# A hybrid SSD and pooling decoder block: the ssd gate as four Strassen pairs, adaLN rows called in other stages, four more warm-up matmuls

## The chip, the cores and the metric

One core of one Trainium2 chip runs the whole block. The metric is the device time of one execution in microseconds, the median of three runs. Beside it there is the profile of one execution, whose span is a little shorter than its own device time.

## What is computed

One decoder block on a sequence of 512 tokens with 1024 channels, all in float32. Cut to what matters here:

```python
mod = silu(c) @ w_ada + b_ada                       # 6 x 1024: shift, scale, gate, twice
h = rmsnorm(x) * (1 + scale_m) + shift_m
z, xbc, dt, u_pool, gate_logits = split(h @ w_in)
y = ssd_scan(silu(conv(xbc)), dt) * silu(z)         # 4 groups, chunks of 128 tokens
y_ssd = group_rmsnorm(y) @ w_branch_ssd
y_pool = causal_pool(u_pool) @ w_branch_pool
g_ssd, g_pool = split(sigmoid(gate_logits))
x = x + gate_m * ((g_ssd * y_ssd + g_pool * y_pool) @ w_out)
h = rmsnorm(x) * (1 + scale_f) + shift_f
x = x + gate_f * (relu(h @ w_up)**2 @ w_down)
out = rmsnorm(x)
```

The gates are 2 x 1024 columns of `h @ w_in`: "the pool gate" and "the ssd gate" below. They are the two halves of the last part of `w_in`.

## The kernel before, in words

Everything is kept transposed: a tile has 128 channels on the partitions and the 512 tokens along the row. Each float32 operand is split into `hi` and `lo` (both float32r): ScalarE copies `hi` (L125, L145, L833), VectorE subtracts `lo` (L126, L146, L834). A product is then three matmuls, hi·hi, hi·lo and lo·hi, in `mm3` (L155, L156, L157). A `unit` makes one output tile of 128 channels: 8 blocks of K times 3 matmuls of 512 columns, 24 in all. Its weights come by `load_unit` (L140 to L146): one DMA of 512 KB on SP's queue into one of 4 `RAW` buffers, then a cast and a subtraction into two of the `HL` buffers.

The stages, in order on TensorE:

1. **First norm** (L200 to L333, an order written out by hand). 12 warm-up matmuls (`warm`, L215 to L221) run while x arrives; two float32 matmuls (L242) broadcast silu(c); three (L251) sum the squares of x; five more warm-up matmuls follow; then the first eight output tiles are summed for each arriving block of h (L321, L327). On the way from the sums to the first L327 lie ScalarE's L295 and L296 (the reciprocal root), VectorE's L312 and ScalarE's L315. `ada(j)` (L171) is one row of `silu(c) @ w_ada`: a DMA of 512 KB from `adaT` and one product-sum on VectorE. Rows 0 to 15 are made here.
2. **Scan**, groups 0 to 3. `run` interleaves the steps of one group's scan with `unit`s that fill TensorE: the convolution's inputs of the next group (`u_x`, `u_bc`, `u_z`) and the branch product of the group before (`bs`, four loads and eight output tiles). At a group's end its y is normalised by L595 and split by L126. Group 3 is filled with the pooling inputs (`pool_in`, L630 to L634) and `pool_mix`.
3. **Pool gate**: 8 units with a sigmoid (L702); after the fourth come `bs(3, i)`, which need the y of group 3, and the second `pool_mix`.
4. **Pool branch**: 8 units of `w_branch_pool`, each multiplied onto the gate (L719).
5. **Ssd gate**: 8 units of h with a sigmoid (L727), times the branch sum (L729), plus the pool part (L730), split (L126) into `mg`.
6. **Output projection**: 8 units of `w_out` on `mg` (five whole, three in halves of 256 tokens), the residual (L759), the second norm in halves (L776, L805 to L807).
7. **MLP** in four quarters. The last three quarters of `w_up` are already done as Strassen pairs (`class Pair`, L886; its matmuls are L892): two output tiles together by seven products of 4 blocks of K times 3 matmuls of 256 columns, 84 matmuls in place of 48 of 512 columns. `prepare` (L853) makes a pair's weight sums on VectorE: four additions of 512 columns, three subtractions of 1024 and one of 512 for `lo`. `sums` (L835) makes the sums of the moving side. L924 and L930 add in PSUM.

The 32 remaining rows of adaLN (16 to 47) are `ada_next` calls: one after each pool gate, one after each `bs(3, i)`, two after each pool branch unit, and the last four in the ssd gate.

A scheduler orders each engine's queue from the program; loads under `urgent` are pulled ahead. Each queue then runs strictly in the order given: on VectorE a waiting instruction holds all behind it. Buffers rotate: a `RAW` buffer's next DMA waits until both the cast and the subtraction (or the L171) that read it are done.

Of the kernel before, what the change touches and what calls it, by code (L numbers as in the profile page):

```python
# [62 lines left out]
def block_kernel(tc, xp, crow, arow, par, adaT, wstart, wz, wx, wpool_in, wgate, wpw, wbs, wbp, wout, wup, wdn, out):  # L63
# [3 lines left out]
    with (  # L67
# [54 lines left out]
        def split(src):  # L122

            hi, lo = S.get(F32R), S.get(F32R)
            act.copy(hi, src)  # L125
            done[0] = dve.tensor_tensor(lo, src, hi.bitcast(F32), ALU.subtract)  # L126
# [98 lines left out]
        with tc.manual_schedule():  # L225
# [17 lines left out]
            HL.put(wide)  # L243
            ps = PU.get()
# [188 lines left out]
        def u_z(g, i):  # L433
            def f():
# [5 lines left out]
                PU.put(ps)  # L440
            return f
# [257 lines left out]
        for j in range(8):
            gp = F.get()  # L700
            ps = unit(wgate[8 + j], h)
            behind(act.activation(gp, ps, AF.Sigmoid))  # L702
            PU.put(ps)
            merged.append(gp)
            if j == 1:
                for _ in rest:
# [16 lines left out]
        mg = []
        for j in range(8):
            gs = F.get()
            ps = unit(wgate[j], h)
            last = act.activation(gs, ps, AF.Sigmoid)  # L727
# [1 line left out]
            dve.tensor_tensor(gs, gs, acc[j], ALU.mult)  # L729
# [7 lines left out]
        free(h)
        with tc.issue_after(last.ins):
            table = act.preload_act_table_set("natural_log_exp_and_others")

        for p_, t in zip((XS, SZ, XS, SZ), later):
            p_.put(t)
        xbig = [XS.get(), XS.get()]
        later = [SZ.get(), SZ.get()]
        F = Slots(lambda i, dt: later[i // 4][:, i % 4, :], 8)


        x1 = []
# [62 lines left out]

# [376 lines left out]
```

## Time and profile before

| | us |
|---|---|
| median of three runs | 967.13 |
| the three runs | 967.13, 965.73, 967.98 |
| the profiled execution's own time | 967.31 |
| its span in the profile | 965.6 |
| TensorE busy | 950.9 |
| VectorE busy | 657.7 |
| ScalarE busy | 500.3 |

A row of the timeline reads: start, duration, engine, line, operation, output<-inputs, size, count, and in brackets the idle time of the engine just before and what ended it. PE is TensorE, DVE VectorE, ACT ScalarE, POOL GpSimd, SP the queue of the DMAs. Matmuls overlap, so their rate is read from the distance of starts and not from one's duration.

### The profile page before, as it was taken

What the parts mean: (1) busy time and instruction counts of PE and PEld (TensorE: products, weight loads), DVE (VectorE), ACT (ScalarE), POOL (GpSimd) and SP (SyncE); (2) the same over time, 40 slices, a digit from 0 to 9 for tenths busy, and PEclk for the clock granted to TensorE, in tenths of its full rate; (3) what the DMA queues carried; (4) which work ended last, traced back from release to release, by engine and by line L of the source; (5) the groups of instructions that cost most, each with busy time, mean ns of one, the idle gap of its engine ahead of it and who ended that gap; (6) DMA issues with size and microseconds to landing.
All of it is one profiled execution on the core that took longest, in us unless ns stands there. A gap on an engine that the chain in (4) does not pass through costs nothing.

```text
span 965.6 us, 13253 instructions
## 1 busy us (share of the span) xinstructions
PE 950.9 (98%) x5131; PEld 803.7 (83%) x5131; DVE 657.7 (68%) x961; ACT 500.3 (52%) x811; POOL 89.7 (9%) x91
## 2 busy tenths in 40 slices
PE   7999999999999999999999999999999999999996
PEld 4877788888888888787888888998899889889986
DVE  7978869567866787987576574795557556664633
ACT  5479976567527642563412452684157137425732
POOL 0102320320312132300000000000000000000000
PEclk9999999999999999999999999999999999999998
DMA  9746333432253333446578453242144225214002
GB/s 355 303 131 181 114 124 118 133 110 94 84 154 116 94 114 126 158 153 202 176 266 270 125 206 113 101 144 68 52 142 132 66 75 165 86 35 152 25 1 88
DMA packets 61761, 129.22 MB, mean 134 GB/s; under 512 B 4673, under 2 KB 29505, under 8 KB 61698
## 3 DMA queue, kind: packets, MB, share of 16 engines
q1 hardware_dynamic: 61696, 128.38, 40.9%
q8 instruction: 40, 0.66, 0.3%
q14 instruction: 23, 0.19, 0.1%
q10 hardware_dynamic: 2, 0.00, 0.0%
HBM read 126.13 MB, written 2.23 MB: 133 GB/s over the span
## 4 chain that ended last, share of the span: by engine, by line
PE 84%; DVE 8%; DMA 3%; ACT 2%; issue 1%; POOL 0%; SPq 0%; DVEq 0%; ACTq 0%; POOLq 0%
PE ps L155 21%; PE ps L156 21%; PE ps L157 21%; PE ps L892 12%; PE ps L327 4%; DMA d<-cs_d 2%; DVE d L146 2%; PE ps L548 1%; DVE s L126 1%; PE ps L528 1%; DMA d<-xp 1%; DVE pad L630 1%; DVE s L396 1%; DVE d L171 1%; PE ps L502 1%
## 5 line engine op out<-in xcount | busy, mean ns | idle before, releaser
L155 PE MATMUL ps<-s,d 128*128 128x512 f32 (+1 forms) x1080 | 412.2, 382 | 1.6 <-ACT sz L438 0.6
L156 PE MATMUL ps<-s,d 128*128 128x512 f32 (+1 forms) x1080 | 408.2, 378 | 0.2 <-DVE s L126 0.2
L157 PE MATMUL ps<-s,d 128*128 128x512 f32 (+1 forms) x1080 | 408.1, 378 | 0.0
L155 PEld LDWEIGHTS ps<-s,d 128*128 128x128 f32 x1080 | 202.6, 188 | 42.9 <-issue 2.1
L157 PEld LDWEIGHTS ps<-s,d 128*128 128x128 f32 x1080 | 202.7, 188 | 38.3 <-issue 0.2
L156 PEld LDWEIGHTS ps<-s,d 128*128 128x128 f32 x1080 | 202.8, 188 | 37.4 <-DVE s L126 0.7
L146 DVE TENSOR_TENSOR d<-d,d 128x1024 fp32r<-128x1024 f32 x88 | 112.2, 1275 | 61.2 <-ACT d L145 56.3
L145 ACT CAST d<-d 128x1024 fp32r<-128x1024 f32 x88 | 92.2, 1048 | 115.6 <-PE ps L156 80.5
L892 PE MATMUL ps<-s,d 128*128 128x256 f32 x864 | 103.8, 279 | 0.0
L892 PEld LDWEIGHTS ps<-s,d 128*128 128x128 f32 x864 | 102.9, 188 | 0.2
L833 ACT CAST d<-d 128x1024 fp32r<-128x1024 f32 x44 | 45.9, 1052 | 88.5 <-PE ps L156 62.7
L834 DVE TENSOR_TENSOR d<-d,d 128x1024 fp32r<-128x1024 f32 x44 | 53.5, 1224 | 27.4 <-ACT d L833 16.8
L833 ACT CAST d<-sz 128x1024 fp32r<-128x1024 f32 x32 | 33.7, 1053 | 68.9 <-PE ps L156 48.9
L1081 DVE SCALAR_TENSOR_TENSOR xs<-ps,mod,xs 128x512 f32<-128x512 f32 x29 | 21.8, 750 | 69.6 <-PE ps L157 69.6
L171 DVE CUSTOM_DVE_ANT_0 d<-d,d,par_t 128x1024 f32<-128x1024 f32 x32 | 41.8, 1306 | 26.7 <-DMA d<-adaT 26.6
L834 DVE TENSOR_TENSOR d<-sz,d 128x1024 fp32r<-128x1024 f32 x32 | 39.2, 1224 | 19.8 <-ACT d L833 18.4
L498 ACT ACTIVATE d<-d,ncs 128x128 f32<-128x128 f32 x128 | 40.0, 393 | 3.6 <-POOL d L494 3.5
L327 PE MATMUL ps<-s,d 128*128 128x512 f32 x168 | 40.1, 391 | 1.6 <-ACT s L315 1.6
L396 DVE SCALAR_TENSOR_TENSOR s<-ps,par_t,s 128x511 f32<-128x511 f32 (+2 forms) x54 | 39.6, 741 | 0.3
L327 PEld LDWEIGHTS ps<-s,d 128*128 128x128 f32 x168 | 31.4, 188 | 9.3 <-ACT s L315 2.1
L125 ACT CAST s<-s 128x512 fp32r<-128x512 f32 x32 | 19.8, 621 | 31.1 <-POOL s L510 18.7
L126 DVE TENSOR_TENSOR s<-s,s 128x512 fp32r<-128x512 f32 x32 | 25.7, 805 | 4.8 <-ACT s L125 4.8
(219 smaller groups left out, 1005.0 us busy)
## 6 DMA issues: line engine op xcount, KB each, us to landing
d<-adaT SPq DMA_DIRECT2D x32, 512.0 KB, 4.1
d<-wx SPq DMA_DIRECT2D x18, 512.0 KB, 3.6
d<-wdn SPq DMA_DIRECT2D x18, 512.0 KB, 3.8
d<-cs_d SPq DMA_DIRECT2D x16, 512.0 KB, 6.0
d<-wbs SPq DMA_DIRECT2D x16, 512.0 KB, 3.5
d<-wgate SPq DMA_DIRECT2D x16, 512.0 KB, 4.4
d<-wz SPq DMA_DIRECT2D x15, 512.0 KB, 3.5
sz<-wdn SPq DMA_DIRECT2D x14, 512.0 KB, 3.9
```

The costliest lines, as they stand in the source:

```text
L145: act.copy(hi[:, :w], r[:, a:a + w])
L146: (low or dve).tensor_tensor(lo[:, :w], r[:, a:a + w], hi[:, :w].bitcast(F32), ALU.subtract)
L155: pe.matmul(ps, whi, xhi[:, t0:t1], start=start, stop=False)
L156: pe.matmul(ps, whi, xlo[:, t0:t1], start=False, stop=False)
L157: pe.matmul(ps, wlo, xhi[:, t0:t1], start=False, stop=stop)
L171: dve.tensor_tensor_reduce(r, r, cbc, 1.0, col("b_ada", j), ALU.mult, ALU.add, mod[:, j:j + 1])
L327: pe.matmul(first[u], w[u][i // 2], h[k][i % 2], start=k == 0 and i == 0, stop=k == 7 and i == 2)
L396: dve.scalar_tensor_tensor(t[:, sh:], ps[:, :T - sh], w(3 - sh), t[:, sh:], ALU.mult, ALU.add)
L498: act.activation(m[:, i, :], m[:, i, :], AF.Exp, bias=ncs[:, c, g * HG + i:g * HG + i + 1])
L833: act.copy(dst[0], src)
L834: dve.tensor_tensor(dst[1], src, dst[0].bitcast(F32), ALU.subtract)
L892: pe.matmul(ps, x, y, start=start and m == 0 and i == 0, stop=m == 3 and i == 2, skip_group_check=True)
```

## The change

**The ssd gate** becomes four Strassen pairs over h. The functions for pairs move up in the file so that the gates can use them; `run_jobs(gates)` runs the four pairs, and the first one's weights are prepared ahead, in the pool branch. Needed for it: the sums of h (`whole`), made from `hi + lo` during the pool branch; `gated`, which does sigmoid, product, sum and split for one output tile; weights of the ssd gate laid out in pairs on the host (`wgs`). Three `HL` buffers more are free from the second pool gate on (the scan's `MT`).

**The adaLN rows** are called elsewhere: one after each `bs` of groups 0 and 1 and after each `u_z` of groups 2 and 3 (16 rows), one after each pool gate (8), two after each of the first whole units of the output projection (8). None is left in the pool branch and in the ssd gate.

**Warm-ups**: `warm(4)` between the broadcast of silu(c) and the sums of squares.

```diff
+            warm(4)
             ps = PU.get()
             sq = [HL.get() for _ in range(4)]
...
+                if g > 1:
+                    ada_next()
...
+                if g < 2:
+                    ada_next()
...
-            ps = unit(wgate[8 + j], h)
+            ps = unit(wgate[j], h)
...
-                F.free += range(12, 16)
+                HL.free += range(8, 11)
...
                 for i in range(4):
                     bs(3, i)()
-                    ada_next()
                 pool_mix(1)()
...
+        def whole(m):
+            us = [U.get(), U.get()]
+            for u, (hi, lo) in zip(us, h[2 * m:2 * m + 2]):
+                dve.tensor_tensor(u, hi.bitcast(F32), lo.bitcast(F32), ALU.add)
...
+            sums(*us, *ts)
+        def gated(p, i, ps, sign):
+            gs = U.get()
+            n = T // len(ps)
+            for i_, part in enumerate(ps):
+                done[0] = act.activation(gs[:, n * i_:n * (i_ + 1)], part, AF.Sigmoid, scale=float(sign))
+            j = 2 * p + i
             dve.tensor_tensor(gs, gs, acc[j], ALU.mult)
             dve.tensor_tensor(gs, gs, merged[j], ALU.add)
...
             mg.append(split(gs))
...
         for j in range(8):
             ps = unit(wbp[j], pout)
             dve.tensor_tensor(merged[j], merged[j], ps, ALU.mult)
             PU.put(ps)
-            ada_next(2)
...
+            if j < 4:
+                ht.append(whole(j))
+            if j == 4:
...
+                hb = moving(h, ht)
+                gates = [Pair(wgs[p], hb, lambda i, ps, sign, p=p: gated(p, i, ps, sign)) for p in range(4)]
+                gates[0].prepare()
...
-        for j in range(8):
-            gs = F.get()
-            ps = unit(wgate[j], h)
-            last = act.activation(gs, ps, AF.Sigmoid)
...
-            if rows:
-                ada_next()
+        run_jobs(gates)
+        last = done[0]
...
             ps = unit(wout[j], mg)
             residual(ps, j, 16)
             PU.put(ps)
+            ada_next(min(2, len(rows)))
```

What this does to the queues, at three places. First TensorE's queue at the first norm; L242 is the broadcast of silu(c), L251 (now L252) the sums of squares, L220 a warm-up. Before:

```order
L242 MATMUL ps_18_128<-d_17_125,ones 128x512
L242 MATMUL ps_19_129<-d_17_125,ones 128x512
L251 MATMUL ps_20_132<-d_22_134,ones 128x512
L251 MATMUL ps_20_132<-d_23_135,ones 128x512
L251 MATMUL ps_20_132<-d_24_136,ones 128x512
L220 LDWEIGHTS s_6_85
L220 MATMUL ps_25_153<-s_6_85 128x512
```

Now:

```order
L242 MATMUL ps_18_128<-d_17_125,ones 128x512
L242 MATMUL ps_19_129<-d_17_125,ones 128x512
L220 LDWEIGHTS s_6_85
L220 MATMUL ps_20_132<-s_6_85 128x512
...
L252 MATMUL ps_21_137<-d_23_139,ones 128x512
L252 MATMUL ps_21_137<-d_24_140,ones 128x512
L252 MATMUL ps_21_137<-d_25_141,ones 128x512
```

Four warm-ups stand ahead of the sums; nothing else of TensorE's order moves before the ssd gate.

Second, VectorE's queue just ahead of the normalising of group 3's y (L595, now L600) in the pool gate; L634 (L639) is the last step of a pooling input, L171 an adaLN row, L146 a weight's `lo`. Before:

```order
L171 ISA d_714_3990,mod<-d_714_3990,d_5_82,par_t 128x1024
L171 ISA mod 128x1
L126 TENSOR_TENSOR s_651_3657<-s_642_3618,s_650_3656 128x512
L630 TENSOR_TENSOR pad_648_3652<-pad_649_3653 128x521
L630 TENSOR_TENSOR pad_649_3653<-pad_648_3652 128x513
L146 TENSOR_TENSOR d_693_3848<-d_691_3845,d_692_3847 128x1024
L632 TENSOR_TENSOR pad_649_3653<-pad_649_3653,par_t 128x16
L634 SCALAR_TENSOR_TENSOR s_652_3665<-pad_649_3653,pad_647_3651 128x512
L126 TENSOR_TENSOR s_661_3703<-s_652_3665,s_660_3702 128x512
L146 TENSOR_TENSOR d_699_3885<-d_697_3882,d_698_3884 128x1024
L595 SCALAR_TENSOR_TENSOR sz_451_2631<-sz_451_2631,par_t,s_670_3748 128x512 x3
```

Now, with L865, L696 to L699 and L692 as steps of `whole`:

```order
L639 SCALAR_TENSOR_TENSOR s_669_3718<-pad_666_3706,pad_664_3704 128x512
L146 TENSOR_TENSOR d_710_3901<-d_708_3898,d_709_3900 128x1024
L146 TENSOR_TENSOR d_720_3969<-d_718_3966,d_719_3968 128x1024
L699 SCALAR_TENSOR_TENSOR pad_772_4265<-pad_772_4265 128x256
L865 TENSOR_TENSOR pad_777_4308<-s_48_259,s_49_260 128x512
L126 TENSOR_TENSOR s_678_3756<-s_669_3718,s_677_3755 128x512
L692 TENSOR_TENSOR xs_672_3722<-pad_772_4265,xs_672_3722 128x512
...
L146 TENSOR_TENSOR d_715_3935<-d_713_3932,d_714_3934 128x1024
L171 ISA d_751_4124,mod<-d_751_4124,d_5_82,par_t 128x1024
...
L600 SCALAR_TENSOR_TENSOR sz_464_2672<-sz_464_2672,par_t,s_687_3801 128x512 x3
```

The first sums of h have moved ahead of the bs(3) products, and one adaLN row stands directly ahead of the normalising. From the pooling inputs of group 3 to this point there were eight L171 and there are five.

Third, VectorE's queue in the ssd gate. Before, one unit's rows:

```order
L146 TENSOR_TENSOR d_844_4738<-d_842_4735,d_843_4737 128x1024
L729 TENSOR_TENSOR xs_655_3669<-xs_655_3669,s_276_1583 128x512
L730 TENSOR_TENSOR xs_655_3669<-xs_655_3669,xs_653_3667 128x512
L126 TENSOR_TENSOR s_821_4612<-xs_655_3669,s_820_4611 128x512
L146 TENSOR_TENSOR d_850_4776<-d_848_4773,d_849_4775 128x1024
```

Now, in the second pair, while the third's weights are made (L727 to L733 additions, L692 `lo`; L881 and L882 the product and sum of a gate; L777 the addition in PSUM):

```order
L881 TENSOR_TENSOR pad_846_4707<-pad_846_4707,s_264_1522 128x512
L881 TENSOR_TENSOR pad_849_4728<-pad_849_4728,s_266_1537 128x512
L777 TENSOR_TENSOR ps_831_4575<-ps_845_4681,pad_803_4448 128x256
L882 TENSOR_TENSOR pad_846_4707<-pad_846_4707,xs_670_3720 128x512
L882 TENSOR_TENSOR pad_849_4728<-pad_849_4728,xs_670_3720 128x512
L727 TENSOR_TENSOR d_854_4738<-d_852_4736 128x512
L126 TENSOR_TENSOR s_848_4713<-pad_846_4707,s_847_4712 128x512
L783 TENSOR_TENSOR ps_845_4681<-ps_845_4681,pad_803_4448 128x256
L126 TENSOR_TENSOR s_851_4733<-pad_849_4728,s_850_4732 128x512
L728 TENSOR_TENSOR d_852_4736<-d_852_4736,pad_855_4739 128x512
...
L692 TENSOR_TENSOR d_857_4746<-d_852_4736,d_856_4745 128x1024
```

The first piece of the third pair's weights (L728, a cast, L692) now stands behind both gates of the first pair. On TensorE the products of the first pair are drawn ahead of most of the last pool branch unit, and parts of the first two output projection units are drawn in between the products of the last pair.

More of the change, by code (lines that the diff above doesn't have):

```diff
@@ L737, in block_kernel @@
[L737 to L748, printed above, removed]
-        for j in range(8):
-            x1.append(xbig[j // 4][:, j % 4, :])
-            if j % 2:
-                sp.dma_start(xbig[j // 4][:, j % 4 - 1:j % 4 + 1, :].rearrange("p a b -> p (a b)"), xp[j // 2])
@@ L770, in block_kernel @@
-        sq = []
-        def norm(t0, t1, sqs, R):
-            ps = PU.get()
-            for i, s in enumerate(sqs):
-                pe.matmul(ps[:, t0:t1], ones, s[:, t0:t1], start=i == 0, stop=i == len(sqs) - 1)
-            with tc.issue_after(table.ins):
-                act.activation(R[:, t0:t1], ps[:, t0:t1], AF.Ln, bias=eps_t, scale=1.0 / DM)
-                act.activation(R[:, t0:t1], R[:, t0:t1], AF.Exp, scale=-0.5)
-            PU.put(ps)
-        for j in range(5):
-            ps = unit(wout[j], mg)
-            residual(ps, j, 16)
-            PU.put(ps)
@@ new lines, in block_kernel @@
+        free(pout)
+        banks = [slots("ps", 1, (P, T), psp, first=4 + i).get() for i in range(4)]
+        BE = Slots(lambda i, dt: (banks[2 * i], banks[2 * i + 1]), 2)
+        AC = slots("ps", 2, (P, T), psp)
+        PU.free = [2, 3]
+        run_jobs(gates)
+        last = done[0]
+        free([t for m in ht[2:] for t in m])
+        PU.free = [2, 3, 0, 1, 4, 5, 6, 7]
+        free(h)
+        with tc.issue_after(last.ins):
+            table = act.preload_act_table_set("natural_log_exp_and_others")
@@ new lines, in block_kernel, with norm @@
+        sq = []
+        def norm(t0, t1, sqs, R):
+            ps = PU.get()
+            for i, s in enumerate(sqs):
+                pe.matmul(ps[:, t0:t1], ones, s[:, t0:t1], start=i == 0, stop=i == len(sqs) - 1)
+            with tc.issue_after(table.ins):
+                act.activation(R[:, t0:t1], ps[:, t0:t1], AF.Ln, bias=eps_t, scale=1.0 / DM)
+                act.activation(R[:, t0:t1], R[:, t0:t1], AF.Exp, scale=-0.5)
+            PU.put(ps)
+        for j in range(5):
+            ps = unit(wout[j], mg)
+            residual(ps, j, 16)
+            PU.put(ps)
+            ada_next(min(2, len(rows)))
@@ new lines, in block_kernel @@
+        free(mg)
+        normed = done[0]
+        for p_, t in zip((SZ, SZ), later):
+            p_.put(t)
+        raws = [SZ.get(), SZ.get()]
+        RAW = Slots(lambda i, dt: D(i, dt) if i < 4 else
+                    raws[i // 2 - 2][:, 2 * (i % 2):2 * (i % 2) + 2, :].rearrange("p a b -> p (a b)"), 8)
+        RAW.free = RAW.free[:4]
+        HL = Slots(lambda i, dt: D(NRAW + i, dt, 48), 12)
+        HL0 = Slots(lambda i, dt: D(NRAW + i, dt), 12)
+        HL0.free = HL.free
+        banks = [slots("ps", 1, (P, T), psp, first=4 + i).get() for i in range(4)]
```

211 lines of the change are left out of this document (110 added, 101 removed).

## The prediction

> **What bounds the kernel now.** I read the page's busy times first, then TensorE's waits, then a table of stages, then the timeline at the places that the change touches.
>
> ```profile
> PE 950.9 (98%) x5131; PEld 803.7 (83%) x5131; DVE 657.7 (68%) x961; ACT 500.3 (52%) x811; POOL 89.7 (9%) x91
> PE ps L327 <- ACT s L315: 1.6, 1, 1.6
> PE ps L251 <- DVE d L257: 1.5, 1, 1.5
> PE ps L155 <- ACT s L648: 0.6, 1, 0.6
> PE ps L156 <- DVE s L126: 0.2, 1, 0.2
> 140.00:320.00 180.00, 180.00 (x930) 148.47 (x929) 122.59 (x180) 111.05 (x195) 33.74 (x34) 1.00 0.38 114
> 373.00:437.00 64.00, 63.15 (x305) 51.22 (x304) 57.96 (x89) 35.27 (x49) 15.14 (x10) 1.00 0.46 148
> 526.50:570.00 43.50, 43.50 (x193) 36.02 (x193) 25.71 (x32) 16.92 (x24) 0.00 (x0) 1.00 0.52 170
> ```
>
> TensorE is the bound: 98% busy, and its waits are short and few. The window rows read: stretch, its length, then busy time of PE, weight loads, DVE, ACT, POOL, the granted clock, DMA share, GB/s. In the scan (140 to 320) and in the ssd gate (526.5 to 570) TensorE never rests, while VectorE is busy 122.59 of 180 and 25.71 of 43.5 us. Only from 373 to 437, around the pooling inputs and the first `bs(3)`, is VectorE nearly full, 57.96 of 64. So a removed matmul counts in full where nothing else comes late, and the question is what VectorE does with what it is given.
>
> **The gate's matmuls.** One unit of the plain gate is the distance of its sigmoids, and a Strassen pair is read from the MLP:
>
> ```profile
> 538.63 0.59 ACT L727 ACTIVATE xs<-ps 128x512 f32<-128x512 f32 x1
> ...
> 560.39 0.59 ACT L727 ACTIVATE sz<-ps 128x512 f32<-128x512 f32 x1
> 872.25 39.64 PE ps L892 x336
> ```
>
> Four units take 560.39 - 538.63 = 21.76 us, 5.44 each, so the eight take 43.52. Four pairs in the MLP, 336 matmuls of 256 columns, take 39.64 on the chain. The gain on TensorE is 43.52 - 39.64 = 3.88 us, provided that it is fed as in the MLP. The order shows it fed differently, which comes next.
>
> **What VectorE has to do for a pair.** These are its operations there, and the spacing of a queue that has work waiting:
>
> ```profile
> L834 DVE TENSOR_TENSOR d<-sz,d 128x1024 fp32r<-128x1024 f32 x12 | 14.7, 1224 | 7.6 <-ACT d L833 7.1
> L870 DVE TENSOR_TENSOR sz<-sz,pad 128x512 f32<-128x512 f32 x3 | 2.1, 693 | 0.1
> L924 DVE TENSOR_TENSOR ps<-ps,pad 128x256 f32<-128x256 f32 x4 | 1.7, 426 | 0.0
> 565.95 1.23 DVE L146 TENSOR_TENSOR d<-d,d 128x1024 fp32r<-128x1024 f32 x1 [1.50 <-ACT d L145]
> 567.10 1.29 DVE L146 TENSOR_TENSOR s<-d,s 128x512 fp32r<-128x512 f32 x2
> 568.30 0.69 DVE L729 TENSOR_TENSOR sz<-sz,s 128x512 f32<-128x512 f32 x1
> 570.40 0.69 DVE L126 TENSOR_TENSOR s<-sz,s 128x512 fp32r<-128x512 f32 x1 [0.69 <-ACT s L125]
> ```
>
> Back to back, one of 1024 columns starts the next after 567.10 - 565.95 = 1.15 us, two of 512 take 568.30 - 567.10 = 1.20, so 0.60 each; one of 256 I put at 0.33 (0.426 less the same 0.09). Weights of a pair: four additions 2.4, three `lo` of 1024 3.45, one of 512 0.6; two additions in PSUM 0.66; two gates of product, sum and `lo` 3.6. Together 10.7 us, against 39.64 / 4 = 9.91 on TensorE. In the MLP the same pair has only two `lo` of 512 in place of the gates, 8.3 us, and keeps up. The first pair's weights are made in the pool branch and the second's additions too; the third's and the fourth's fall inside the stretch, behind earlier gates in VectorE's queue. In those two pairs VectorE falls 10.7 - 9.9 = 0.8 us behind if it never rests, and 12.1 - 9.9 = 2.2 by the rows' durations without the overlap (2.77 + 3.67 + 0.69 + 0.85 + 4.16). It does rest a little: the queue stops at each addition in PSUM until TensorE is there, and a `lo` waits for its `hi` (0.69 in the last row). I take 1.05 a pair, near the back-to-back figure because at both places work stands ready, so 2.1 us of the 3.88 are lost. The ends are 0 (TensorE's order has filler products of `w_out` between the last pair's) and 4.5 (two pairs at 2.2). Net of the gate: -1.8.
>
> ScalarE has, per pair, casts and sigmoids under 8 us and stays free. The end of the gate is covered: 24 matmuls of the second `w_out` unit stand ahead of the last blocks of `mg`. The sums of h (two additions, two subtractions of 512 and four of 256: 2.4 + 1.3 = 3.7 us each, four times) replace adaLN rows in the pool branch and cost nothing there.
>
> **The warm-ups.** The start, with the clock in the last but two column of the windows:
>
> ```profile
> 9.05 1.10 PE L251 MATMUL ps<-d,ones 128*128 128x512 f32 x2 [1.46 <-DVE d L257]
> 10.45 3.48 PE L251 MATMUL ps<-d,ones 128*128 128x512 f32 x4 [0.31 <-DVE d L248]
> 16.91 0.50 PE L327 MATMUL ps<-s,d 128*128 128x512 f32 x1 [1.63 <-ACT s L315]
> 7.54:10.95 3.41, 1.65 (x4) 0.59 (x4) 2.58 (x4) 2.34 (x4) 0.00 (x0) 1.00 1.02 395
> 10.96:14.37 3.41, 3.41 (x6) 0.96 (x5) 3.26 (x6) 2.28 (x4) 0.00 (x0) 0.50 1.03 417
> 14.37:17.78 3.41, 1.78 (x8) 0.93 (x7) 2.57 (x6) 3.15 (x5) 0.58 (x1) 1.00 1.03 420
> 11.11 0.69 DVE L248 TENSOR_TENSOR d<-d 128x512 f32<-128x512 f32 x1
> 13.22 1.28 DVE L171 CUSTOM_DVE_ANT_0 xs<-xs,d,par_t 128x1024 f32<-128x1024 f32 x1
> 13.97 0.69 ACT L295 ACTIVATE s<-ps,eps_t 128x512 f32<-128x512 f32 x1 [1.10 <-PE ps L251]
> 15.35 0.75 DVE L312 SCALAR_TENSOR_TENSOR s<-d,amod,s 128x512 f32<-128x512 f32 x1 [0.84 <-ACT s L296]
> ```
>
> From 10.96 to 14.37 the granted clock was 0.50, after a stretch in which TensorE was busy 1.65 of 3.41 us (48%); after one of 1.78 (52%) it stayed at 1.00. The last two records of L251 wait for the addition that ends at 11.80 and at half clock end at 13.93; at full clock half of that, about 12.8. Four warm-ups of about 0.21 add some 0.8 us to the first stretch, 2.4 of 3.41, well over 52%, so I expect the clock to stay. L295 then starts 1.1 earlier, but L312 also waits behind L171 until 13.22 + 1.28 = 14.50, so it gains the 0.84 that VectorE waits. The first L327 comes 0.84 earlier, and TensorE is the bound from there. Ends: 0 and -1.1. The value is the row's 0.84.
>
> [...]
>
> **The adaLN rows.** An L171 is 1.2 us of VectorE. Sixteen go to the scan, 16 x 1.2 = 19 us into a VectorE idle for 180 - 122.6 = 57 of 180 us: 0, with up to +1 for a row that waits for its DMA. Eight go beside the output projection, 9.6 us into 27: 0, up to +1. Ahead of group 3's normalising there are five instead of eight:
>
> ```profile
> 422.49 0.69 DVE L634 SCALAR_TENSOR_TENSOR s<-pad,pad 128x512 f32<-128x512 f32 x1
> 429.26 2.08 DVE L595 SCALAR_TENSOR_TENSOR sz<-sz,par_t,s 128x512 f32<-128x512 f32 x3 [3.21 <-ACT s L589]
> 435.64 0.69 DVE L126 TENSOR_TENSOR s<-sz,s 128x512 fp32r<-128x512 f32 x1 [0.69 <-ACT s L125]
> ```
>
> L634 comes about 4 us earlier (four L171 less by then, one weight `lo` moved behind it, some 3 us of sums of h ahead of it). Between it and L600 now stand some 8 us where 6.8 - 3.2 = 3.6 were. L600 starts where ScalarE lets it, 0.7 earlier because the 0.6 us wait for L648 goes, but the last L126 stands behind one more L171 (+0.3). Net -0.4, ends -0.8 and +0.8. TensorE then still waits for that L126.
>
> **The sum**, against the profiled execution's 967.31: -3.88 + 2.1 - 0.84 - 0.4 = -3.0, so 964.3. The median of the runs is 0.18 below the profiled execution; I say 964.2.
>
> **The rivals.**
> (1) All is hidden, as in the MLP, where TensorE hardly waits: -3.88 - 0.84 - 0.4 = -5.1, so 962.0 (the rivals' times too are less the 0.18). Against it stands 10.7 over 9.9. Chance 0.22.
> (2) VectorE stays behind through the gate: the upper end of 4.5 us, so -3.88 + 4.5 - 0.84 - 0.4 = -0.6, 966.5. For it speaks that a product, a sum and a `lo` follow each other with 0.69 us waits. Chance 0.16.
> [...] Chance 0.12.
> (4) Slower: an L171 in the scan holds VectorE's queue until its DMA lands.
>
> ```profile
> DVE d L171 <- DMA d<-adaT: 26.6, 16, 4.6
> 153.89 1.21 DVE L499 TENSOR_TENSOR d<-d,ps 128x1024 f32<-128x1024 f32 x1
> 161.39 1.09 PE L548 MATMUL ps<-d,s 128*64 128x128 f32 x16
> ```
>
> Sixteen of them waited 26.6 us before, 1.66 each, harmless where they stood. In the scan, L499 ends 161.4 - 155.1 = 6.3 us before TensorE needs it. Four L171 ahead of it cost 4.8 us and, with such waits, 11.4: 5.1 us late, at the start of groups 1 and 2 both, so +10, less 3.0: 974. It decides from a mean wait of 0.4 us a row, if VectorE's idle time there doesn't take it. Against it: the DMA share is 0.38 in the scan against 0.5 to 0.7 later. Chance 0.07.
>
> **How the numbers follow.** My forecast has 0.43 and reaches from 963 to 965.6. The range runs from (1) to the far side of (2), 961.9 to 967.0; it leaves out (4) and the edges. 0.2%, about what a measurement of this kernel can tell from no change, is 1.9 us, so faster means under 965.2. Most of the forecast (0.36), all of (1) and half of (3) lie there: 0.64. Slower is (4) and a little of (2): 0.08. The rest, 0.28, is the same.
>
> **What would show it.** In the changed profile: the clock at 1.00 from 11 to 14 us and the first L327 near 16.1; VectorE without idle time in the second and third pairs, and TensorE's waits there for L692 or L728's cast, about 1 us twice; L892's successor at about 0.118 us a matmul; `bs(3)` waiting about 2 us for L126; no TensorE wait in the scan. The prediction is wrong if the stage takes under 40.5 us or over 44, if the clock falls at the start all the same, or if TensorE waits in groups 1 and 2.

## The result and the profile after

The changed kernel takes 979.47 us (median of five, 977.20 to 981.37) against 967.13 before: ratio 1.0131, interval 1.0118 to 1.0145. It is 12.3 us slower where I had forecast 2.9 faster. The profiled execution took 978.15 us, its span is 976.4.

The page's busy times, and the largest waits of TensorE (what it waited for, us in total, times, longest):

```profile
PE 951.4 (97%) x5279; PEld 810.0 (83%) x5279; DVE 689.7 (71%) x1025; ACT 517.0 (53%) x843; POOL 90.8 (9%) x91
```

```profile
PE ps L950 <- DVE sz L941: 5.1, 1, 5.1
PE ps L156 <- DVE s L126: 3.1, 3, 1.5
PE ps L155 <- DVE s L397: 2.9, 2, 2.5
...
PE ps L745 <- DVE d L692: 0.5, 1, 0.5
...
PE ps L745 <- ACT d L691: 0.5, 1, 0.5
PE ps L745 <- ACT ps L772: 0.4, 1, 0.4
```

VectorE has 689.7 - 657.7 = 32 us more to do, and the three largest waits of TensorE name VectorE. Where the time went can be read by comparing when the same matmul starts in the two profiles. The lines L155 to L157 give 3420 matmuls before and 3228 after; up to the wbp units both run in the same order, so I count them from the first, and behind the gate from the last. The difference of the starts, stage by stage, is a ledger of the change (us, + is later than before):

| run (one profiled execution each) | start | scan | pool_mix(0) | bs(3) | last wbp, gate, first w_out | second norm | rest | sum |
|---|---|---|---|---|---|---|---|---|
| changed kernel | -1.1 | +4.8 | -0.9 | +2.1 | -0.8 | +7.1 | -0.4 | +10.8 |
| e1, rows off w_out | +0.5 | +5.0 | -0.9 | +2.0 | +0.9 | 0.0 | +0.3 | +7.8 |
| e2, rows off the scan | -1.6 | -0.8 | -0.9 | +2.1 | -0.6 | +5.6 | -0.5 | +3.2 |
| e3, rows as before | -2.1 | +0.2 | 0.0 | +3.8 | +3.0 | 0.0 | +0.2 | +5.2 |
| e4, before with warm-ups | -2.1 | +0.3 | 0.0 | 0.0 | 0.0 | 0.0 | +0.2 | -1.8 |
| e5, rows without loads | -0.8 | +4.4 | -0.9 | +3.1 | -0.8 | +0.1 | +0.2 | +5.2 |
| e6, rows with short sums | -0.8 | +1.1 | -0.9 | +2.1 | +1.7 | +1.4 | +0.3 | +4.8 |
| e7, rows late in a group | -0.5 | +4.0 | -0.9 | +2.2 | +0.3 | +0.4 | +0.2 | +5.7 |
| e9, as e7, sums held | -2.3 | +3.0 | -0.9 | +0.5 | +0.7 | 0.0 | +0.3 | +1.2 |
| e10, as e9, gates on GpSimd | -2.4 | +2.9 | -0.9 | 0.0 | +13.3 | 0.0 | +0.2 | +13.0 |
| e11, as e12, gates on GpSimd | -1.8 | -0.4 | -0.9 | +0.2 | +16.4 | 0.0 | 0.0 | +13.5 |
| e12, no scan rows, sums held | +0.6 | -0.2 | -0.9 | -0.4 | +1.8 | +0.3 | +0.3 | +1.5 |
| e13, before with the new rows | -0.4 | +4.2 | -0.9 | -0.8 | +5.6 | +0.7 | +0.2 | +8.6 |
| e14, as e12, gate sums left out | -1.2 | +0.4 | -0.9 | +0.1 | +1.1 | 0.0 | +0.3 | -0.3 |
| e15, as e12, one more slot | -2.3 | -0.1 | -0.9 | +0.1 | +2.5 | +0.2 | +0.2 | -0.2 |
| e16, as e12, last gates first | -2.5 | -0.3 | -0.9 | -0.1 | +2.9 | 0.0 | -0.1 | -0.9 |
| e17, e15 and e16 together | +0.4 | +0.2 | -0.9 | -0.1 | +2.1 | 0.0 | +0.2 | +1.9 |

Each column ends at the same matmul: the first L155 (60.0 us before), the end of the scan (378.2), after pool_mix(0) (400.5), after bs(3) (438.1), inside the second w_out unit (579.9), after the second norm (613.0), the last one (956.5). In the changed kernel the scan and the second norm add 11.9, and all the rest together takes 1.1 off. A row is one execution and can lie off its run's median: e13's is the slowest of nine (976.68, median 972.52), e9's the fastest of seven (968.52, median 970.44). So the ledger tells where time went, and the medians tell how much.

**The scan.** VectorE's queue around the start of group 2, and the matmul that waits:

```profile
243.04 1.29 DVE L171 CUSTOM_DVE_ANT_0 d<-d,d,par_t 128x1024 f32<-128x1024 f32 x1 [2.47 <-DMA d<-adaT]
...
245.85 1.21 DVE L504 TENSOR_TENSOR d<-d,ps 128x1024 f32<-128x1024 f32 x1
...
256.54 1.28 DVE L171 CUSTOM_DVE_ANT_0 d<-d,d,par_t 128x1024 f32<-128x1024 f32 x1
...
258.88 0.74 DVE L397 SCALAR_TENSOR_TENSOR s<-ps,par_t,s 128x511 f32<-128x511 f32 x1
...
260.71 0.74 DVE L397 SCALAR_TENSOR_TENSOR s<-ps,par_t,s 128x509 f32<-128x509 f32 x1
```

```profile
261.60 0.47 PE L155 MATMUL ps<-s,d 128*128 128x512 f32 x1 [2.48 <-DVE s L397]
```

Four rows of 1.2 us stand in 20 us of this queue, and one of them waits 2.47 for its load. The decay product L504 and the convolutions L397 come behind them, and TensorE needs a PSUM buffer that L397 frees. The windows around this start, before and then changed (the third busy time is VectorE's):

```profile
235.00:262.00 27.00, 27.00 (x143) 22.31 (x142) 20.35 (x28) 12.91 (x21) 7.19 (x6) 1.00 0.31 98
```

```profile
235.00:265.00 30.00, 27.10 (x141) 21.82 (x140) 25.63 (x38) 13.71 (x21) 3.35 (x3) 1.00 0.52 172
```

**The second norm.** VectorE, then ScalarE, of the changed kernel; then SP's queue in the changed kernel and before:

```profile
607.79 0.48 DVE L933 SCALAR_TENSOR_TENSOR xs<-ps,mod,xs 128x256 f32<-128x256 f32 x1
612.10 1.23 DVE L692 TENSOR_TENSOR d<-d,d 128x1024 fp32r<-128x1024 f32 x1 [3.83 <-ACT d L691]
613.24 0.42 DVE L941 TENSOR_TENSOR sz<-sz,sz 128x256 f32<-128x256 f32 x1
...
616.97 0.42 DVE L941 TENSOR_TENSOR sz<-sz,sz 128x256 f32<-128x256 f32 x1 [0.48 <-ACT sz L940]
```

```profile
611.02 1.05 ACT L691 CAST d<-d 128x1024 fp32r<-128x1024 f32 x1 [3.87 <-DMA d<-wup]
```

```profile
588.25 2.47 SPq L170 DMA_DIRECT2D d<-adaT  x2
592.14 0.33 SPq L1019 DMA_DIRECT2D d<-wup  x1
```

```profile
568.41 0.38 SPq L981 DMA_DIRECT2D d<-wup  x1
```

The adaLN loads take turns with the weights in the four RAW buffers. The first w_up load goes out at 592.1, where it went at 568.4 before. A later one lands at 610.9; the split of that weight (L692) stands ahead of the norm's last sums (L941) in VectorE's queue, so a weight of the MLP that is not needed yet makes the norm late. TensorE then waits 5.07 us at L950, and the clock falls:

```profile
611.38:614.79 3.41, 1.00 (x9) 0.80 (x7) 2.69 (x4) 1.96 (x3) 0.00 (x0) 1.00 0.13 24
614.79:618.20 3.41, 0.75 (x3) 0.66 (x3) 1.64 (x5) 0.83 (x2) 0.00 (x0) 0.50 0.78 256
618.20:621.62 3.42, 3.42 (x17) 3.33 (x16) 1.89 (x5) 2.19 (x5) 0.00 (x0) 0.50 0.08 29
```

The last but two column is the granted clock: 0.50 until 621.6, in which I see the rest of the 7.1 us.

### The profile page after: what moved, and what is told of

It reads as the page before. It is cut to its first block, busy times and chain, and to the rows that moved or that the text cites. A ratio compares the mean times of both kernels' runs of the same rounds, so it can differ in the third digit from the quotient of the medians.

```text
span 976.4 us, 13664 instructions
## 1 busy us (share of the span) xinstructions
PE 951.4 (97%) x5279; PEld 810.0 (83%) x5279; DVE 689.7 (71%) x1025; ACT 517.0 (53%) x843; POOL 90.8 (9%) x91
## 4 chain that ended last, share of the span: by engine, by line
PE 64%; DVE 16%; DMA 8%; ACT 7%; issue 3%; POOL 1%; SPq 0%; DVEq 0%; POOLq 0%; ACTq 0%
PE ps L156 15%; PE ps L157 15%; PE ps L155 15%; PE ps L745 14%; PE ps L328 4%; DMA d<-cs_d 4%; DVE d L146 3%; DVE s L126 2%; ACT d L145 2%; DMA d<-adaT 2%; DVE s L397 1%; DVE d L171 1%; DMA d<-wout 1%; DVE d L692 1%; ACT d L503 1%
## 5 line engine op out<-in xcount | busy, mean ns | idle before, releaser
L155 PE MATMUL ps<-s,d 128*128 128x512 f32 (+1 forms) x1016 | 386.8, 382 | 3.6 <-DVE s L397 2.9
L156 PE MATMUL ps<-s,d 128*128 128x512 f32 (+1 forms) x1016 | 383.4, 378 | 1.6 <-DVE s L126 1.6
L157 PE MATMUL ps<-s,d 128*128 128x512 f32 (+1 forms) x1016 | 383.7, 378 | 0.0
L155 PEld LDWEIGHTS ps<-s,d 128*128 128x128 f32 x1016 | 190.5, 188 | 42.7 <-issue 5.7
L156 PEld LDWEIGHTS ps<-s,d 128*128 128x128 f32 x1016 | 190.9, 188 | 36.7 <-DVE s L126 2.3
L157 PEld LDWEIGHTS ps<-s,d 128*128 128x128 f32 x1016 | 190.7, 188 | 35.7 <-issue 0.2
L146 DVE TENSOR_TENSOR d<-d,d 128x1024 fp32r<-128x1024 f32 x80 | 103.1, 1290 | 50.5 <-ACT d L145 25.6
L745 PE MATMUL ps<-s,d 128*128 128x256 f32 x1080 | 132.2, 280 | 0.0
L745 PEld LDWEIGHTS ps<-s,d 128*128 128x128 f32 x1080 | 129.9, 188 | 0.4
L145 ACT CAST d<-d 128x1024 fp32r<-128x1024 f32 x80 | 83.3, 1044 | 65.3 <-PE ps L157 20.9
L691 ACT CAST d<-d 128x1024 fp32r<-128x1024 f32 x56 | 58.3, 1050 | 99.1 <-PE ps L156 63.5
L692 DVE TENSOR_TENSOR d<-d,d 128x1024 fp32r<-128x1024 f32 x56 | 68.0, 1224 | 39.1 <-ACT d L691 23.3
L691 ACT CAST d<-sz 128x1024 fp32r<-128x1024 f32 x32 | 33.6, 1051 | 68.8 <-PE ps L156 48.9
L171 DVE CUSTOM_DVE_ANT_0 d<-d,d,par_t 128x1024 f32<-128x1024 f32 x32 | 42.7, 1335 | 15.3 <-DMA d<-adaT 15.3
L692 DVE TENSOR_TENSOR d<-sz,d 128x1024 fp32r<-128x1024 f32 x32 | 39.2, 1224 | 19.7 <-ACT d L691 18.4
L397 DVE SCALAR_TENSOR_TENSOR s<-ps,par_t,s 128x511 f32<-128x511 f32 (+2 forms) x54 | 39.7, 742 | 0.2
L328 PEld LDWEIGHTS ps<-s,d 128*128 128x128 f32 x168 | 31.4, 188 | 9.6 <-ACT s L316 2.4
L125 ACT CAST s<-s 128x512 fp32r<-128x512 f32 x32 | 19.7, 618 | 25.4 <-POOL s L515 20.2
L126 DVE TENSOR_TENSOR s<-s,s 128x512 fp32r<-128x512 f32 x32 | 25.7, 803 | 9.2 <-ACT s L125 9.2
```

The lines of the kernel that those rows point to most:

```text
L145: act.copy(hi[:, :w], r[:, a:a + w])
L146: (low or dve).tensor_tensor(lo[:, :w], r[:, a:a + w], hi[:, :w].bitcast(F32), ALU.subtract)
L155: pe.matmul(ps, whi, xhi[:, t0:t1], start=start, stop=False)
L156: pe.matmul(ps, whi, xlo[:, t0:t1], start=False, stop=False)
L157: pe.matmul(ps, wlo, xhi[:, t0:t1], start=False, stop=stop)
L171: dve.tensor_tensor_reduce(r, r, cbc, 1.0, col("b_ada", j), ALU.mult, ALU.add, mod[:, j:j + 1])
```

## The experiments

Every run was timed beside the kernel before on the same chip; the ratio is given with its interval. The ledger above has the profiles of e1 to e17; there is no e8.

### Where the rows stand: e1 to e4

e1 and e2 take the rows out of one stage, e3 out of both; each adds them to the wbp units. e4 is the kernel before with `warm(4)`.

```diff
# e1
-            ada_next(min(2, len(rows)))      # behind each w_out unit
+            ada_next()                       # behind each wbp unit
# e2
-                if g > 1: ada_next()         # in u_z
-                if g < 2: ada_next()         # in bs
+            ada_next(2)                      # behind each wbp unit
```

> The changed kernel with the eight adaLN rows beside the output projection moved ahead, one behind each wbp unit; all else as changed. Theory (the rows' 512 KB loads stand between the w_out and w_up loads, and VectorE's queue waits for a late weight): TensorE's 5.1 us wait at the second norm goes and the 1.3 us at half clock behind it too, so 979.5 - 6.7 = 972.8. Rival (the norm is late because VectorE comes late out of the Strassen gate, whatever the rows do): the wait stays over 4 us, 978 to 980.

> The changed kernel with the sixteen adaLN rows of the scan moved to the wbp units, two behind each; the eight beside the output projection stay. Theory (a row in the scan holds VectorE's queue until its load is there, and the load takes a place ahead of the next weight): TensorE's waits at the start of the second and third group (1.5 and 2.9 us and what follows, 4.8 us by the matmuls' start times) go, 0.8 comes back at the first pool_mix, so 979.5 - 4.0 = 975.5. Rival (the groups are late for another reason than the rows): 979.

> The changed kernel with Strassen gate and warm-ups, but with no adaLN row in the scan or beside the output projection: eight at the pool gates, four behind the bs(3) units, twenty behind the wbp units. Theory (the rows' places are the whole loss): before's 967.1 less 1.1 at the start and 0.7 net in the gate, 965.3; up to 967 if VectorE, with the sums of h, the first pair's weights and twenty rows in the wbp units, comes late into the gate. Rival (the Strassen gate or the sums of h cost more than they bring wherever the rows stand): 968 or more.

> The kernel before with only the four warm-ups added. Theory: the clock stays at 1.00 between 11 and 14 us and the first matmul of the first projection comes 1.1 us earlier, 967.1 - 1.1 = 966.0. Rival (the warm-ups fall otherwise in the clock's windows in other executions, or the norm's chain on ScalarE sets the start anyway): 967.1, no change.

e1: 975.98, ratio 1.0111 (1.0090 to 1.0131). The wait at the second norm is gone (+7.1 becomes 0.0). Two things take half of it back: TensorE now waits 1.6 us for the last split of `mg` (why is read at e16), and the profiled start was 1.6 later by the clock (below). e2: 971.34, 1.0054 (1.0039 to 1.0069): the scan goes from +4.8 to -0.8, more than forecast. e3: 974.89, 1.0088 (1.0070 to 1.0106): my 965.3 was wrong. Without a row in either stage 5.2 us remain: 3.8 at bs(3), and 3.0 in the stage of the gate, 1.7 of them by the last wbp unit, which waits for its own weights (twenty rows stand in VectorE's queue in that stage). So the rows' places are not the whole loss. e4: 966.52, 1.0002 (0.9994 to 1.0011): the warm-ups bring 1.8 in one profile and nothing in the median.

### Load or VectorE's time: e5 and e6

Both take a price of the row apart, and both leave the 24 sums out of the result: e5 keeps VectorE's work and drops the load, e6 keeps the load and sums 64 of 1024 columns.

```diff
# e5, for the 24 rows of the scan and of w_out
-            sp.dma_start(r, adaT[j])
-            dve.tensor_tensor_reduce(r, r, cbc, ...)
+            dve.tensor_tensor_reduce(r, cbc, cbc, ...)
# e6, for the same rows
-            dve.tensor_tensor_reduce(r, r, cbc, ...)
+            dve.tensor_tensor_reduce(r[:, :64], r[:, :64], cbc[:, :64], ...)
```

> The changed kernel with every adaLN row in its place, but the 24 rows of the scan and of the output projection's stage load nothing: they take their slot of the ring and work on the broadcast vector that lies there already (so their sums are left out). VectorE does the same work at the same places. Theory (what a row costs there is its load: the wait for it in VectorE's queue and its place ahead of the next weight): the waits at the second and third group and at the second norm go, 979.5 - 4.0 - 6.7 = 968.8, up to 971 if the wait of 1.8 us for the last blocks of mg comes up as in the run with the rows off the output projection. Rival (it is VectorE's 1.2 us a row): 979, no change.

> The changed kernel with every row and every load in its place, but the 24 rows of the scan and of the output projection's stage multiply 64 columns where 1024 were (the rest of their sums is left out), so that VectorE is spared about 24 x 1.1 = 26 us there. Theory (the loads): within 2 us of the changed kernel, 977.5 to 979.5, and the three waits stay above 1 us each. Rival (VectorE's time): 969 to 971.

e5: 972.65, 1.0066 (1.0053 to 1.0079). e6: 973.60, 1.0076 (1.0059 to 1.0092). Neither theory holds for both stages. TensorE's waits in e5, then in e6:

```profile
PE ps L156 <- DVE s L126: 4.3, 3, 1.9
...
PE ps L155 <- DVE s L399: 1.2, 1, 1.2
```

```profile
PE ps L156 <- DVE s L126: 2.1, 3, 1.0
...
PE ps L956 <- DVE sz L947: 1.3, 1, 1.3
...
PE ps L155 <- DVE s L399: 0.6, 1, 0.6
```

In the scan the rows cost 4.4 of 4.8 without any load, and 1.1 with the loads but short sums: it is VectorE's time that counts there, and my theory of the loads falls. At the second norm no load means no wait (0.1), and the loads with short sums leave 1.4 of 7.1. So neither alone makes the 7.1: it takes the loads, and with them the 1.2 us of each row. By the program a RAW buffer is free for the next load only when its row is done, which would be the link; no run isolates it. In e6 the stage ahead is also 2.5 us later, so the 1.4 is no clean price. And it is not the first w_up load that counts: in e5 it goes out at 593.6, later than in the changed kernel, and TensorE does not wait.

### The same rows without Strassen, and rows late in a group: e13, e7, e9, e12

e13 is the kernel before with plain gates and only the rows moved. e7 is the changed kernel with rows left at the u_z units and the pool gates; the rest goes to the wbp units. e9 adds a hold of the sums of h; e12 is e9 without scan rows.

```diff
# e9 and e12; normal is the last subtraction of group 3's normalising
-                ht.append(whole(j))
+                with tc.issue_after(normal.ins):
+                    ht.append(whole(j))
```

> The kernel before, plain gates and no new warm-ups, with only the adaLN rows at the changed kernel's places: sixteen in the scan, eight at the pool gates, eight beside the output projection. Theory (the rows' places are the loss, without Strassen too): 4 us in the scan and 5 to 7 at the second norm, 976 to 978. Rival (the rows hurt only beside the Strassen gate's work and weights): 967 to 970.

> The changed kernel with the eight rows behind the bs units of the scan and the eight beside the output projection moved to the wbp units, two behind each; the eight behind the u_z units and at the pool gates stay. Theory (rows hurt where a group's start or the norm stands behind them, and the u_z units stand late in a group): the run with no row in the scan gave 971.3; less its 5.0 us at the second norm, plus 1.8 for the last blocks of mg, 968.1. Rival (any row in the scan costs the same, 4.8 / 16 each): 970.5.

> As the run with the rows late in the group, and the sums of h held in VectorE's queue until the last split of group 3's normalising is issued. Theory (the sums and their casts, hoisted between the pooling inputs, make the chain of ScalarE and VectorE to bs(3) late: 1.9 us in the changed kernel): 1.5 to 1.9 us under that run, 966.4. Rival (one more row in front of the last L126 is what makes bs(3) late, or the held sums push the first pair's weights into the gate): no gain, 968 or more.

> The same places of the rows and the sums held, with the gate's products and sums on VectorE as in the changed kernel. Theory: 2.4 less than the run with the sums held, 968.0; so about 1.5 over the kernel before, which is what the Strassen gate then costs in all. Rival: 970 or more.

e13: 972.52, 1.0054 (1.0035 to 1.0074), with nine runs from 967.05 to 976.68. The scan's +4.2 is there without Strassen. Beside the output projection the rows cost 5.6 at another place: TensorE waits 3.7 us for the last split of the plain gates, and the clock is at half for 6.8 us behind it. ScalarE there:

```profile
581.48 1.14 ACT L145 CAST s<-d 128x512 fp32r<-128x512 f32 x2 [4.95 <-DMA d<-wout]
582.53 0.61 ACT L125 CAST s<-sz 128x512 fp32r<-128x512 f32 x1
```

The split's cast (L125) stands behind the cast of a w_out weight that waits 4.95 us for its load. It is the order of loads again, by way of another queue. e7: 971.37, 1.0049 (1.0031 to 1.0066): the eight u_z rows alone cost 4.0, late in group 2 (2.1 at 293 us of the kernel before, 0.9 at 321). So where they stand in a group did not save them, and my theory falls; but the rival's equal price a row (4.8 / 16) would be 2.4. At 293 TensorE waits 1.72 us for VectorE's L543, and ahead of that ScalarE waits 3.49 for the load of `cs_d`, so not all of it need be VectorE's time. e9: 970.44, 1.0039 (1.0025 to 1.0053), intervals that overlap with e7's; but bs(3) falls from +2.2 to +0.5 in the ledger, and it stays between -0.4 and +0.2 in every later run with the sums held. The chain there, on ScalarE, before and changed:

```profile
424.70 0.58 ACT L702 ACTIVATE xs<-ps 128x512 f32<-128x512 f32 x1
425.30 1.28 ACT L588 ACT_TABLE_LOAD   x1
```

```profile
427.66 0.62 ACT L691 CAST pad<-pad 128x512 fp32r<-128x512 f32 x1
428.18 1.05 ACT L145 CAST d<-d 128x1024 fp32r<-128x1024 f32 x1
429.13 0.59 ACT L846 ACTIVATE xs<-ps 128x512 f32<-128x512 f32 x1
429.74 1.28 ACT L593 ACT_TABLE_LOAD   x1
```

The table load for the normalising comes 4.4 us later, TensorE only 2.8: casts of the sums (L691), which need VectorE's sums, stand ahead of the sigmoid and the table. With the sums held back the load comes at 425.13 again (e9). e12: 967.68, 1.0015 (1.0001 to 1.0029): with the rows and the sums out of the way, the change is a tie at best.

### Where the gate's 3.9 us went: e10, e11, e14, e15, e16, e17

In every profile with Strassen the gate's stage comes out at -0.8 or more. In the changed kernel three waits, with the slower matmuls that restart behind them (0.15 to 0.22 us from start to start, then 0.12 again), make 2.2 of the 3.1 us that are lost, by the distances of the matmuls' starts; the other 0.9 are ten steps of 0.05 to 0.13. The three waits, and the windows of the stage ahead of them and around them:

```profile
552.68 0.51 PE L745 MATMUL ps<-xs,d 128*128 128x256 f32 x2 [0.46 <-ACT d L691]
...
553.95 0.39 PE L745 MATMUL ps<-xs,d 128*128 128x256 f32 x1 [0.52 <-DVE d L692]
...
557.05 0.62 PE L745 MATMUL ps<-xs,d 128*128 128x256 f32 x3 [0.45 <-ACT ps L772]
```

```profile
526.50:546.00 19.50, 19.50 (x142) 18.26 (x141) 6.75 (x9) 5.98 (x11) 0.00 (x0) 1.00 0.14 41
546.00:557.00 11.00, 9.62 (x77) 9.02 (x75) 11.00 (x18) 6.67 (x12) 0.00 (x0) 1.00 0.24 72
```

VectorE is busy 6.75 of the first 19.5 us and 11.00 of the next 11: it idles first, and then everything falls due at once.

e10 gives the gate's products and sums of three pairs to GpSimd, e11 does so without scan rows. e14 leaves them out of the computation. e15 adds a slot for the pairs' weights. e16 puts the last pair's gate ahead of the later w_out weights, e17 is e15 and e16 together.

```diff
# e10, e11
+            e = pool if p < 3 else dve
-            dve.tensor_tensor(gs, gs, acc[j], ALU.mult)
-            dve.tensor_tensor(gs, gs, merged[j], ALU.add)
+            e.tensor_tensor(gs, gs, acc[j], ALU.mult)
+            e.tensor_tensor(gs, gs, merged[j], ALU.add)
# e15, behind the last wbp unit
+        HL.free.insert(0, 11)
# e16: the last pair's product, sum and split under high_priority, and
-        w = [load_unit(wout[j], at=S, cols=T) for j in (5, 6, 7)]
+        with tc.issue_after(tail[0].ins):
+            w = [load_unit(wout[j], at=S, cols=T) for j in (5, 6, 7)]
```

> As the run with the sums held, and for the first three Strassen pairs of the gate the product and the sum (L881, L882 of the changed kernel) go from VectorE to GpSimd, which is idle there: VectorE is spared four additions of 0.60 us a pair, 2.4 of 10.7. Theory (VectorE is late in the gate by its amount of work): the three waits of TensorE in the gate (3.2 us with the slow matmuls behind them) shrink to under 1, 2 to 3 us less than the run with the sums held, 968. Rival (VectorE is late because the next pair's weights wait for their load and for slots, while it idles 9 us in the first pair): 970.4, no change. GpSimd slower than thought, or in VectorE's way: 971 or more.

> As the run before it in this list, with no row in the scan either: one behind each of the first four pool gates, two behind each of the last four, three behind each of the first four wbp units, two behind the last four. Theory (the u_z rows cost the third group 2.4 to 3 us): 2.4 less than the run before it in this list, 965.5, under the kernel before. Rival (twenty rows in the wbp units make the first pair's weights late, as in the run with the rows as before): 968.

> As the run with no row in the scan and the sums held (967.7), but the gate's sixteen products and sums on VectorE are left out of the computation, 1.2 us a gate, 2.4 of the 10.7 us a pair. Theory (VectorE's amount of work between the pairs is what TensorE waits for): the three waits of 0.45 to 0.52 us in the gate and the one for the last blocks of mg (1.2 us) go, the gate brings its 3.9, so 967.7 - 3.2 - 1.2 = 963.3. Rival (the next pair's weights wait for slots and loads, VectorE idles before it is late): the three waits stay, 966.5.

> As the run with no row in the scan and the sums held, with a twelfth slot for the parts of the pairs' weights (the broadcast vector's, free after the last row), taken first by the second pair. Theory (VectorE's amount of work): the same waits, 967.7. Rival (slots): VectorE works ahead in the first pair, the three waits go, 964.5 to 965.5.

> As the run with no row in the scan and the sums held; the last pair's product, sum and split come ahead of the later w_out weights in VectorE's queue. Theory (behind the gate TensorE waits 1.2 us for the last split because six parts of w_out's last units stand ahead of it): that wait falls to 0.2, 966.7. Rival (the chain of sigmoid, product, sum, cast and lo is that long by itself): 967.7.

> The two before it together: by the rival on slots and the theory on the last split 963.5 to 964.5, under the kernel before; by the theory on VectorE's amount of work 966.7.

e10: 981.49, 1.0159 (1.0139 to 1.0179); e11: 979.81, 1.0142 (1.0121 to 1.0162). The stage of the gate got 13 to 15 us longer (e10 against e9, e11 against e12) instead of 3 shorter. VectorE while GpSimd works, then GpSimd, in e10:

```profile
540.67 1.78 DVE L725 TENSOR_TENSOR d<-d 128x512 f32<-128x512 f32 x1
542.37 1.75 DVE L690 TENSOR_TENSOR pad<-pad,pad 128x512 fp32r<-128x512 f32 x1
```

```profile
539.90 2.00 POOL L881 TENSOR_TENSOR pad<-pad,s 128x512 f32<-128x512 f32 x1 [126.03 <-ACT pad L878]
541.98 1.59 POOL L882 TENSOR_TENSOR pad<-pad,xs 128x512 f32<-128x512 f32 x1
```

An addition that takes VectorE 0.69 alone takes 1.78 beside GpSimd, and the split of a gate waits for GpSimd's slow result. So these two runs say nothing on VectorE's amount of work.

e14 does: 967.25, 1.0012 (1.0001 to 1.0023). Its largest waits:

```profile
PE ps L157 <- DVE d L146: 2.2, 1, 2.2
...
PE ps L741 <- DVE ps L773: 0.9, 1, 0.9
```

The three waits are gone, so less work for VectorE is enough to remove them. But a wait of 0.9 for an addition in PSUM has come up, and the last wbp unit waits 2.2 for its `lo` (1.2 in e12). Of the +1.1 of the stage, 2.5 is at that last unit by the ledger's matmul starts, so the gate alone is at -1.4: of 3.88, still only 1.4 are kept with 9.6 us of VectorE's work left out (8 gates of two times 0.6). By the distances of the matmuls' starts the other 2.4 are 1.1 at that addition, 0.5 at a split of `mg` and 0.8 in small steps. e15: 968.99, 1.0030 (1.0018 to 1.0042): one slot more also removes the three waits from their places (one of 0.3 for L768 is left, in the first pair), by letting VectorE work ahead, and 0.9 and 1.7 for other things take their place. So the slots are not out: the waits go with less work and go with one more slot. e16: 967.43, 1.0013 (1.0003 to 1.0023), with 1.3 at the last split as before, although the products and splits did move ahead of the `lo`s in VectorE's queue. ScalarE shows what else stands there:

```profile
571.58 1.15 ACT L145 CAST s<-d 128x512 fp32r<-128x512 f32 x2 [0.80 <-DMA d<-wout]
572.63 0.86 ACT L876 ACTIVATE pad<-ps 128x256 f32<-128x256 f32 x2
```

The gate's last matmul starts at 571.63, and its sigmoids (L876) wait behind a cast of a w_out weight that came late; in e1 and e12 it is the same. No run moves that cast, so this reading is not shown by an experiment. e17: 967.15, 1.0012 (1.0001 to 1.0023). None of the runs e10 to e17 beats the kernel before. What stays open is how much of the gain a schedule with VectorE free in time could keep.

### The start: e18 and e19

Four warm-ups took 2 us off one profile and nothing off the median. The first matmul of the projection starts between 14.46 and 15.90 us in the profiles with the warm-ups; but e13 and e19, which are without the four, start it at 14.95 and 14.63, so the 16.91 of the kernel before was its one profiled execution. The stretch from that matmul to the first L155 takes 43.1 us in most profiles and 44.7 in seven. The windows of e12, one of the seven:

```profile
13.08:16.49 3.41, 1.50 (x8) 0.70 (x6) 3.41 (x6) 3.19 (x5) 0.30 (x1) 1.00 1.03 422
16.49:19.91 3.42, 3.42 (x10) 2.68 (x9) 3.42 (x7) 0.61 (x3) 0.36 (x1) 0.50 1.03 415
```

The steps of the clock, 3.41 us apart, lie elsewhere from execution to execution: one is at 14.37 us before, at 15.51 in e13 and at 16.49 in e12. In e12 one window held the 1.9 us idle stretch ahead of the first projection, and the next ran at half clock, 1.6 us lost. The changed kernel's own profile had the windows so that both stretches passed. In e9 (the second fence; e10 and e16 are alike) they passed too, with the whole 1.9 us stretch in one window:

```profile
10.63:14.04 3.41, 2.96 (x9) 0.79 (x7) 3.26 (x6) 3.20 (x5) 0.00 (x0) 1.00 1.04 420
14.04:17.46 3.42, 1.66 (x7) 1.40 (x8) 3.42 (x6) 2.36 (x4) 0.67 (x1) 1.00 1.02 418
```

```profile
11.28:14.69 3.41, 1.51 (x7) 0.50 (x5) 3.38 (x7) 3.01 (x6) 0.00 (x0) 1.00 1.04 420
14.69:18.11 3.42, 3.42 (x15) 2.82 (x16) 3.42 (x7) 1.09 (x2) 0.67 (x1) 1.00 1.02 411
```

So TensorE's busy time in a window does not decide alone: 1.50 was followed by half clock in e12, and 1.51 by full clock in e9. What else decides stays open.

e18 is the kernel before with four warm-ups ahead of the norm's sums and thirteen instead of five behind them; e19 has only the thirteen.

```diff
-            warm(5)
+            warm(13)
```

> The kernel before with the four warm-ups ahead of the sums and thirteen instead of five behind them, so that TensorE's idle 1.9 us before the first matmul of the projection shrinks to 0.2. Theory (a 3.4-us window of the clock that falls on an idle stretch gives the next window at half clock, and the windows' place differs from execution to execution: the four warm-ups only cover the earlier stretch): no window cools at the start in any execution, first L155 matmul near 57.7 in place of 57.5 to 60.6, 966.2 - 1.5 = 964.7. Rival (the start is not what the runs differ by): 966.2, no change.

> The kernel before with only the thirteen warm-ups behind the sums. Theory: the earlier stretch still cools in some executions, so between, 965.5. Rival: 966.2, no change.

e18: 965.88, 0.9996 (0.9986 to 1.0006); e19: 965.44, 0.9992 (0.9983 to 1.0001). The median hardly moves, but the runs draw together: 965.31 to 967.04 in e18 and 964.52 to 966.51 in e19, beside 963.97 to 968.46 for the kernel before on the same chip. The mean granted clock that each execution has on record bears it out: of the kernel before's 21 executions twelve have 0.996 and take 967.27 us in the mean, seven have 0.998 and take 965.18, and none of the 22 of e18 and e19 is under 0.997. So the clock goes with a good part of the spread between executions. Both medians are under the kernel before, neither clear of no change.

## Why the prediction was wrong, point by point

- **The adaLN rows: the step that failed.** I wrote "19 us into a VectorE idle for 180 - 122.6 = 57 of 180 us: 0" and for the output projection "9.6 us into 27: 0, up to +1". The profile has +4.8 and +7.1. I took a stage's idle share for slack. In the changed kernel VectorE is busy 12.01 of 20 us at the end of group 1 (215 to 235) and 25.63 of 30 around the start of group 2, and TensorE waits for what stands behind the rows there. e2 shows that the rows are the cost (rows off, cost off), e5 and e6 show that in the scan it is VectorE's time. TensorE waiting in groups 1 and 2 was one of my own signs of being wrong.
- **Rival (4)** had the right place, the starts of groups 1 and 2, but the wrong mechanism for most of it (a load that holds the queue) and a price of 10 instead of 4.8. I gave it 0.07. The second norm was in no rival: I counted the rows' VectorE time there, and not their eight loads of 512 KB in the four RAW buffers that w_up's weights share.
- **The sums of h "cost nothing there".** They cost 1.7 of the 2.2 at bs(3), by e9 against e7 (one profile each; the medians are 0.9 apart and their intervals overlap). My -0.4 for bs(3) saw the right matmul wait (0.95, 0.41 and 0.66 us for L126 and its cast) but left out that the sums' casts stand in ScalarE's queue ahead of the table load.
- **The wait for L648** goes, as forecast (-0.9 at pool_mix(0)).
- **The gate.** The -3.88 is right for TensorE's matmuls, and the lateness of VectorE sits about where I put it, at the third pair's weights. But my way to it, 10.7 us of work over 9.9 of TensorE, missed that VectorE idles 12.8 us at the head of the stage. The size: 2.1 forecast; in the changed kernel the stage gives -0.8, so 3.1. That this is near is partly luck: my term had no slots and no restarts in it. In e1, e9 and e12, without the rows beside the output projection, the last split of mg costs 1 to 1.6 more, which I had called covered.
- **The warm-ups.** The clock stayed at 1.00 and the first L155 came 1.1 earlier, at the end of my range (0 to 1.1). Over executions the gain is nil (e4, ratio 1.0002): the clock's stretches lie elsewhere from one profile to another (the start's stretch takes 43.1 us in most, 44.7 in seven).

## What to carry to other kernels

Idle share of an engine over a stage is not slack: ask which instruction of that engine is waited for next, and what will stand ahead of it in the queue, and count every moved step's load as well as its arithmetic. When an engine that is not the bound is asked for 32 us more, moving the work about moves the wait about: each placement of the rows that was tried here made something else late. Removing matmuls pays only as far as the engines that feed them can work ahead.

## What the runs showed of the hardware

- **The clock's windows.** A half-clock stretch at the start began at 10.96 us before, at 15.51 in e13 and at 16.49 in e12; in the 3.41 or 3.42 us ahead of it TensorE was busy 1.65, 1.52 and 1.50. But 1.66 of 3.42 was followed by full clock in the changed kernel, and so was 1.51 of 3.41 in e9. A later wait was followed by it too: behind the 5.1 us at the second norm, with TensorE busy 1.00 of 3.41, the clock was at 0.50 for 6.8 us. The stretches are 3.41 us long before (10.96 to 14.37) and 6.83 at the changed kernel's second norm (614.79 to 621.62).
- **VectorE and GpSimd slow each other.** In e10 three VectorE operations of 512 columns with both inputs in SBUF take 1.78, 1.75 and 1.43 us beside GpSimd (540.67 to 545.81), where such an addition takes 0.69 alone. An addition with an input in PSUM (L775) takes 0.42 there, and its four 0.426 in the mean, as in e9 without GpSimd (0.427). Not every operation with both inputs in SBUF is longer: two L690 of 1024 columns that begin ahead of GpSimd's first product take 2.36 together. GpSimd's products (L881) take 1.74 in the mean. The changed kernel's scan shows both sides: a VectorE L146 of 1024 columns takes 2.12 at 171.96 beside GpSimd and 1.22 in the gate, where GpSimd rests; GpSimd's L578 takes 1.32 at 174.76 beside VectorE's L171 and 0.46 at 215.71 with VectorE idle.
